# One place modulo 256 bytes for all TensorE operands of a two-network kernel, and offsets of their own for two kinds of tiles

## The chip, the cores and the metric

The kernel runs on 1 core of one Trainium2 chip. The metric is the device time of one execution in microseconds (us). Its profile follows five engines: PE is TensorE's matmul (PEld its weight load), DVE VectorE, ACT ScalarE, POOL GpSimd and SP SyncE.

## The reference

Two networks follow each other, both of depth 2 on 512 tokens of width 1024, all in float32. The first has latent attention and differential attention, each followed by a layer norm and a squared-ReLU MLP of width 4096 with a layer norm. The second has forgetting attention and retention, each followed by a SwiGLU MLP of width 2816, with root-mean-square norms ahead of each part.

```python
def reference(x, positions, ...):
    x = first_block(x, positions, ...)
    return second_block(x, norm_mix_2, ...)

def first_block(x, ...):
    for i in range(2):
        m = _mla(x, ...) if i == 0 else _diff_attn(x, ...)
        x = _layernorm(ALPHA * x + m, ...)
        x = _layernorm(ALPHA * x + square(relu(x @ w_up)) @ w_down, ...)
    return x

# second_block, for each of its two layers:
#   x = x + (forgetting_attention or retention)(rmsnorm(x, g1))
#   x = x + (silu(a) * b) @ w_out,  with  a, b = halves of  rmsnorm(x, g2) @ w_in
# and at last rmsnorm(x, final_norm)
```

## The kernel before

The whole program is one instruction stream for each engine. There are eight stages: mla, f0 (MLP), diff, f1 (MLP), fox, g0 (SwiGLU), ret and g1 (SwiGLU).

**Three products for one.** Every float32 operand is split into two float32r parts, a high and a low one (`split`: ACT copies the high part, DVE subtracts it). `mm3` then issues three TensorE products: high times high, high times low, low times high. The first argument of `matmul` after the output is the stationary operand (128 columns that are loaded into the array), the second the moving one (up to 512 columns that stream through).

**Weights** come from DRAM as chunks of [128, 1024] float32 through two `raw` buffers, and are split into a ring of five `whi` and five `wlo` tiles (`get`, `done`).

**Feature-major products** (`fgemm`, `ftile`, `fhead`, `proj`): 128 columns of `whi` or `wlo` are stationary, and the normed tokens `XH` or `XL` (features on partitions, 512 tokens) move. One output tile takes 8 k-tiles of three products. `fhead` does the first four tiles of a stage in halves of 256 tokens: the first halves need the token tiles 0 and 1 alone, the second halves the tiles 2 and 3.

**Token-major products** (`tgemm`, made of `t_first` and `t_second`, and `v_half`): 128 tokens are stationary, 512 columns of a weight chunk move. In an MLP the stationary operands are `jh` and `jl`: `jit` splits two k-tiles of the hidden layer (`h` or `z`) just in time, with 3 buffers in f0 and f1 and 4 in g0 and g1. `t_second` takes most chunks in the order chunk, then token tile. The last `lr` chunks (3 in f0 and f1, 4 in g0 and g1) it takes in the order token tile, then chunk, so that a token tile is finished every 6 `lr` products. Each finished token tile goes through its norm (`ln_fin` or `rms_fin`: `add` and `a` on DVE, ACT and POOL), then through 8 transposes on PE and a split into `XH` and `XL` (`to_xT`), for the `fhead` of the next stage.

**Order.** A list scheduler at build time gives each engine its order: the instruction that comes first in the program among those that are ready. A tile of a pool is handed to a new user when all users of the former one are done. So an instruction that needs a buffer still in use is passed by later ones.

**Where tiles lie.** A tile takes a byte range of its own in every partition, rounded up to 32 bytes, and tiles follow one another in the order of their pools. The sizes of nearly all tiles are multiples of 256 bytes. Exceptions move what comes behind them: `mh` (16 bytes) and `col` (64) lie between `XH`, `XL` and the weight ring; four tiles `ss` of 8 bytes lie ahead of `jh` and `jl` in g0 and g1, and ahead of ret's tiles; three small tiles in diff, and `bf`, `rc` in fox, lie ahead of the attention's tiles. The four `st` tiles of 48 bytes take 256 together.

Of the kernel before, what the change touches and what calls it, by code (L numbers as in the profile page):

```python
# [9 lines left out]
F32 = mybir.dt.float32  # L10
F32R = mybir.dt.float32r
# [4 lines left out]
PSUM = bass.MemoryType.PSUM  # L16

D = 1024
S = 512
NT = 4  # L20
# [8 lines left out]
AUTO = True  # L29
# how much of the tensor engine's other work (ns) is put before what waits for a chain of the  # L30
# other engines, and how many products of that work go with each query tile
PLAN = {
# [8 lines left out]
class Net:  # L41
    def __init__(self, ctx, tc, A):
        self.tc, self.nc, self.A = tc, tc.nc, A
        nc = self.nc
        self.cst = ctx.enter_context(tc.tile_pool(name="cst", bufs=1))
        self.wp = ctx.enter_context(tc.tile_pool(name="wp", bufs=1))
        self.sm = ctx.enter_context(tc.tile_pool(name="sm", bufs=1))
        self.pp = ctx.enter_context(tc.tile_pool(name="pp", bufs=8, space=PSUM))
        c = self.cst
        self.X = c.tile([128, NT, D], F32, name="X")  # L50
        self.XH = c.tile([128, 8, S], F32R, name="XH")
        self.XL = c.tile([128, 8, S], F32R, name="XL")
        self.idn = c.tile([128, 128], F32, name="idn")
        self.mask = c.tile([128, S], F32, name="mask")
        self.mh = c.tile([128, 4], F32, name="mh")
        self.col = c.tile([128, 16], F32, name="col")
        self.seq = []
        self.n_dma = self.n_split = self.n_get = self.n_done = 0
        self.raw, self.sp = {}, {}
        self.fq = []  # L60
        self.unit = 0
        self.rt = self.tables = None
        self.late = {}
        self.owed = 0
        self.clk, self.dq, self.busy = 0.0, [], False

    def ps(self, name="ps"):
        return self.pp.tile([128, 512], F32, tag="ps", name=name)

    def small(self, n, name):  # L70
        return self.sm.tile([128, 8], F32, tag="small", name=name, bufs=24)[:, 0:n]

    # weight stream: every chunk is [128, n] of float32, split into two float32r parts
    def dma_next(self, eng=None):
# [46 lines left out]

    # work behind a chain of the other engines is issued only after enough of the tensor
    # engine's other work: clk counts what the tensor engine was given, in ns
    def defer(self, delay, fn):
# [33 lines left out]

    # features on partitions: out[m, tok] over kts k-tiles, weights stationary
    def fgemm(self, ps, w, off, kts, xh, xl, n0=0, n1=S, m=128):  # L160
# [5 lines left out]

    # the first tiles after a norm run in token halves, so that the norm's tail is hidden
    def fhead(self, n, evac):
# [35 lines left out]
    def mm_t(self, ps, t, lh, ll, w, first, last):  # L204
        # two k-tiles of a [128 tok, 512] product
        ts = slice(t * 128, t * 128 + 128)
        for j in range(2):
            ws = slice(j * 512, j * 512 + 512)
            self.mm3(ps, lh[:, j, ts], ll[:, j, ts], w[0][:, ws], w[1][:, ws], first and j == 0, last and j == 1)

    # tokens on partitions: out[tok, 1024] in two column halves, lhs(c) -> (hi, lo) [128, 2, 512]
    def t_first(self, nch, lhs, fin0, ahead=True):
# [17 lines left out]
    def t_second(self, nch, lhs, lr, fin_a, fin_b, strict, pre=None):  # L230
        fin = []
        b = [self.ps("tb") for _ in range(NT)]
        L = pre or {0: lhs(0)}
# [48 lines left out]

    # one 512-column half of a normed [128, 1024] token tile into xT
    def to_xT(self, src, t, g):
# [56 lines left out]
    def rms_fin(self, pool, g, dst=None):  # L341
        nc = self.nc
        X = [self.halves(self.X[:, t, :]) for t in range(NT)]
        G = self.halves(g)
        ss = [pool.tile([128, 2], F32, name=f"ss{t}", bufs=1) for t in range(NT)]
        out = {}
# [22 lines left out]
    def jit(self, pool, src, bufs, tags=("jh", "jl"), ready=None):  # L369
        def lhs(c):  # L370
            if ready is not None:
                self.need(lambda: ready() > 2 * c + 1)
            h = pool.tile([128, 2, S], F32R, tag=tags[0], name="jh", bufs=bufs)
            l = pool.tile([128, 2, S], F32R, tag=tags[1], name="jl", bufs=bufs)
            self.split(h, l, src[:, 2 * c:2 * c + 2, :])
            return h, l
        return lhs

    # causal softmax numerators of [128 q, keys] in PSUM; sum into rs
    def softmax(self, pool, s, qt, tag, sm, scale=1.0):  # L380
# [22 lines left out]

    # out^T [dv, q] = sum over keys of V^T P^T; V is [tok, head, (tile, dv)], and the result takes
    # the place of its head's values as [dv, head, (tile, q)]
    def pv(self, VH, VL, h, PH, PL):
# [6 lines left out]

    # heads cut into query tiles: scores of one tile, other work for the tensor engine, and the
    # transposes and values behind the chains of the softmax
    def attend(self, pool, heads, scores, VH, VL, post, fills):
# [25 lines left out]

    # rotary embedding with features on partitions; swap names, in each group of 32 partitions, the
    # partner of a feature
    def rope(self, pool, src, swap, C, Sn):
# [8 lines left out]

    # cos and signed sin of positions * inv, features on partitions
    def rope_tables(self, pool, tmp, which, tags=("t0", "t1", "t2"), bufs=1):
# [212 lines left out]

    # attention, its output projection and the norm behind it  # L670
    def attn_out(self, outer, p, scores, VH, VL, nready, post, fills, gname, bname, row):
# [15 lines left out]
    def ffn1(self, i):  # L687
        nc, A, tc = self.nc, self.A, self.tc
        with ExitStack() as es:
            p = es.enter_context(tc.tile_pool(name="f_a", bufs=1))  # L690
            h = p.tile([128, 32, S], F32, name="h")
            g = self.bcast(p, A["ln_ffn_g"][i:i + 1, :], D, "g")
# [9 lines left out]
            for m in range(4, 32):  # L702
                evac(m, self.ftile())
                if m == 8 and i == 0:
                    self.tables = self.rope_tables(self.rt, p, 1, ("ntmp",) * 3, 4)
            self.tgemm(16, self.jit(p, h, 3), 3, self.ln_fin(p, g, bb, g2))

# [6 lines left out]

    # one 512-column half of a token-major projection: 4 chunks of two k-tiles
    def v_half(self, VH, VL, dst):
# [11 lines left out]
    def diff(self):  # L728
        nc, A, tc = self.nc, self.A, self.tc
        mm = nc.tensor.matmul  # L730
        with ExitStack() as outer:
# [3 lines left out]
            p = outer.enter_context(tc.tile_pool(name="d_a", bufs=1))  # L735
            nlam = p.tile([128, 1], F32, name="nlam")
            sub = p.tile([128, 1], F32, name="sub")
            ones = p.tile([128, 2], F32, name="ones")
            with tc.tile_pool(name="d_0", bufs=1) as p0:
# [18 lines left out]
            def evac(h, which):  # L758
                def f(ps):
                    r = self.rope(p, ps, DIFF_SWAP, C, Sn)  # L760
                    # a sub-head's queries lie above their low parts, its keys twice: one product of full
                    # height gives two of the three parts
                    if which == 0:
# [24 lines left out]
            def scores(h, qt):  # L788
# [3 lines left out]
                if qt == 0:  # L792
                    s1[h] = p.tile([128, 4], F32, tag="s1", name="s1", bufs=3)
                q, k, kl = qk[h]
# [18 lines left out]
            def post(h, o):  # L813
# [6 lines left out]
                def sums():  # L820
# [5 lines left out]
                    nc.vector.tensor_copy(s8, sps[:, 0:8])  # L826
                    # the values lack the division by the sum of the first softmax; so does eps
                    nc.vector.tensor_tensor(rr, s1[h], s1[h], op=ALU.mult)
# [19 lines left out]
    def fox(self):  # L848
        nc, A, tc = self.nc, self.A, self.tc
        mm = nc.tensor.matmul  # L850
        with ExitStack() as outer:
# [3 lines left out]
            pa = p = outer.enter_context(tc.tile_pool(name="x_a", bufs=1))  # L855
            bf = p.tile([32, 1], F32, name="bf")
            nc.gpsimd.dma_start(out=bf, in_=A["fox_b"])
            rc = p.tile([32, 16], F32, name="rc")
            nc.gpsimd.dma_start(out=rc, in_=A["c_rows"])
# [194 lines left out]
    def ffn2(self, i):  # L1054
        nc, A, tc = self.nc, self.A, self.tc
        n = DFF2 // 128
        with ExitStack() as es:
# [15 lines left out]
            for m in range(4, 2 * n):  # L1073
                evac(m, self.ftile())
            self.tgemm(n // 2, self.jit(p, z, 4), 4, self.rms_fin(p, g, A["out"] if i == 1 else None))

# [29 lines left out]
def body(tc, A, phases=PHASES, auto=AUTO):  # L1106
    with ExitStack() as ctx:
# [8 lines left out]
        for ph in phases:  # L1116
            net.plan = PLAN[ph]
            if ph in ("f0", "diff") and net.rt is None:
# [23 lines left out]
def pack_v(w):  # L1142
    # 512 columns, two k-tiles a chunk
    return w.reshape(-1, 2, 128, 512).transpose(0, 2, 1, 3).reshape(-1, 128, 1024)


def pack_h(w):
    # two 512-column halves, each in chunks of two k-tiles
    return np.concatenate([pack_v(np.ascontiguousarray(w[:, :512])), pack_v(np.ascontiguousarray(w[:, 512:]))])


# rotary features of the latent attention, the two halves side by side in each group of 32
ROPE_ORDER = np.array([16 * (i // 32) + i % 16 + 32 * (i % 32 // 16) for i in range(64)])
# [110 lines left out]
```

## Time and profile before

| | us |
|---|---|
| median of 2 runs (2596.21 and 2596.28) | 2596.24 |
| span of the profiled execution, first to last instruction | 2594.1 |
| time around that span (median less span) | 2.1 |
| PE busy | 2561.4 |
| DVE busy | 1289.7 |
| ACT busy | 929.4 |
| POOL busy | 170.4 |

Busy time counts a product from its start to its modelled end, and the products overlap: what a product costs in a row of others is the distance from its start to the next one's start, not its duration. The profiled execution's own time outside its span isn't listed, so sums are made in the span and carried over to the median one to one.

### The profile page before, as it was taken

The numbers are of one execution on the slowest core, as the hardware profiler recorded it, in microseconds if no ns is written. First come the engines' busy times: TensorE is split into PE (matmuls) and PEld (weight loads), VectorE is DVE, ScalarE is ACT, GpSimd is POOL, SyncE is SP. The second block draws the span as 40 slices with busy tenths as digits, with TensorE's granted clock in tenths as the row PEclk, the third lists the DMA queues.
The fourth block names the chain that finished last, engine by engine and source line by source line (L and its number), as shares of the span: only waits on it lengthen the run. The fifth ranks groups of instructions, "written<-read, shape, count | busy, mean of one in ns | idle before, by whom it ended". The sixth has DMA issues, their size and how long they took to land.

```text
span 2594.1 us, 30292 instructions
## 1 busy us (share of the span) xinstructions
PE 2561.4 (99%) x12164; PEld 2100.7 (81%) x12164; DVE 1289.7 (50%) x1961; ACT 929.4 (36%) x1416; POOL 170.4 (7%) x238
## 2 busy tenths in 40 slices
PE   8999999999999999999999999999999999999998
PEld 7778888887778888887778888888888888888887
DVE  6865334566986333546455432244455544432243
ACT  5634223335663323334443322233322233322232
POOL 1100000012431000003000000000000000000000
PEclk9999999999999999999999999999999999999999
DMA  4213323323122322232211322222322222322322
GB/s 153 98 49 126 98 90 98 98 76 98 58 65 90 98 98 90 98 98 84 74 57 49 119 93 97 90 96 91 112 77 85 77 82 81 106 98 90 98 90 74
DMA packets 65837, 233.05 MB, mean 90 GB/s; under 512 B 7536, under 2 KB 7680, under 8 KB 65696
## 3 DMA queue, kind: packets, MB, share of 16 engines
q1 hardware_dynamic: 62064, 219.21, 25.8%
q0 software_dynamic: 3488, 11.55, 1.4%
q8 instruction: 95, 1.56, 0.3%
q14 instruction: 46, 0.38, 0.0%
q10 hardware_dynamic: 144, 0.36, 0.0%
HBM read 228.99 MB, written 2.10 MB: 89 GB/s over the span
## 4 chain that ended last, share of the span: by engine, by line
PE 54%; POOL 0%; issue 0%; ACT 0%; DVE 0%; DVEq 0%; POOLq 0%; ACTq 0%
PE ps L151 8%; PE ps L152 8%; PE ps L150 8%; PE ta L150 2%; PE ta L152 2%; PE ta L151 2%; PE tb L152 2%; PE tb L151 2%; PE tb L150 2%; PE pj L150 2%; PE v L150 2%; PE v L152 2%; PE pj L152 2%; PE pj L151 2%; PE v L151 2%; PE tp L156 1%
## 5 line engine op out<-in xcount | busy, mean ns | idle before, releaser
L117 DVE TENSOR_TENSOR wlo<-raw,whi 128x1024 fp32r<-128x1024 f32 (+2 forms) x415 | 507.6, 1225 | 535.1 <-ACT whi L116 530.5
L116 ACT CAST whi<-raw 128x1024 fp32r<-128x1024 f32 (+2 forms) x415 | 431.4, 1041 | 878.2 <-PE ps L151 578.5
L150 PE MATMUL ps<-XH,whi 128*128 128x512 f32 (+1 forms) x1664 | 609.7, 367 | 2.1 <-ACT XH L116 2.1
L151 PE MATMUL ps<-XL,whi 128*128 128x512 f32 (+1 forms) x1664 | 608.8, 366 | 0.2 <-DVE XL L117 0.2
L152 PE MATMUL ps<-XH,wlo 128*128 128x512 f32 (+1 forms) x1664 | 608.5, 366 | 0.0
L150 PEld LDWEIGHTS ps<-XH,whi 128*128 128x128 f32 x1664 | 314.2, 189 | 57.7 <-ACT XH L116 2.3
L151 PEld LDWEIGHTS ps<-XL,whi 128*128 128x128 f32 x1664 | 314.4, 189 | 56.0 <-DVE XL L117 0.7
L152 PEld LDWEIGHTS ps<-XH,wlo 128*128 128x128 f32 x1664 | 314.3, 189 | 55.8
L150 PE MATMUL ta<-whi,jh 128*128 128x512 f32 x496 | 194.6, 392 | 0.0
L152 PE MATMUL ta<-whi,jl 128*128 128x512 f32 x496 | 194.3, 392 | 0.0
L151 PE MATMUL ta<-wlo,jh 128*128 128x512 f32 x496 | 194.3, 392 | 0.0
L150 PE MATMUL tb<-whi,jh 128*128 128x512 f32 x448 | 176.5, 394 | 0.0
L152 PE MATMUL tb<-whi,jl 128*128 128x512 f32 x448 | 175.6, 392 | 0.0
L151 PE MATMUL tb<-wlo,jh 128*128 128x512 f32 x448 | 175.6, 392 | 0.0
L117 DVE TENSOR_TENSOR jl<-h,jh 128x1024 fp32r<-128x1024 f32 x64 | 78.4, 1225 | 174.8 <-ACT jh L116 174.8
L116 ACT CAST jh<-h 128x1024 fp32r<-128x1024 f32 x64 | 67.6, 1056 | 205.7 <-PE ta L151 110.8
L150 PE MATMUL pj<-XH,whi 128*128 128x512 f32 x288 | 121.2, 421 | 0.0
L152 PE MATMUL pj<-XH,wlo 128*128 128x512 f32 x288 | 114.3, 397 | 0.0
L151 PE MATMUL pj<-XL,whi 128*128 128x512 f32 x288 | 113.8, 395 | 0.0
L152 PEld LDWEIGHTS ta<-whi,jl 128*128 128x128 f32 x496 | 93.3, 188 | 20.6
L151 PEld LDWEIGHTS ta<-wlo,jh 128*128 128x128 f32 x496 | 93.3, 188 | 20.3
L150 PEld LDWEIGHTS ta<-whi,jh 128*128 128x128 f32 x496 | 93.3, 188 | 20.3
(325 smaller groups left out, 3612.2 us busy)
## 6 DMA issues: line engine op xcount, KB each, us to landing
raw<-in_w_in SPq DMA_DIRECT2D x88, 512.0 KB, 3.3
raw<-in_w_up SPq DMA_DIRECT2D x64, 512.0 KB, 3.3
raw<-in_w_dn SPq DMA_DIRECT2D x64, 512.0 KB, 3.3
raw<-in_w_r SPq DMA_DIRECT2D x48, 512.0 KB, 3.3
raw<-in_w_out SPq DMA_DIRECT2D x44, 512.0 KB, 3.3
raw<-in_w_d SPq DMA_DIRECT2D x24, 512.0 KB, 3.3
raw<-in_w_x SPq DMA_DIRECT2D x24, 512.0 KB, 3.3
raw<-in_w_ro SPq DMA_DIRECT2D x16, 512.0 KB, 3.3
```

The lines of the kernel that those rows point to most:

```text
L116: nc.scalar.copy(hi, src)
L117: (eng or nc.vector).tensor_tensor(lo, src, hi.bitcast(F32), op=ALU.subtract)
L150: mm(ps, ah, bh, start=first, stop=False)
L151: mm(ps, ah, bl, start=False, stop=False)
L152: mm(ps, al, bh, start=False, stop=last)
L156: self.nc.tensor.transpose(out, src, self.idn)
```

## The change

It does four things.

1. Tiles whose size is no multiple of 256 bytes are padded or gathered, so that all tiles that TensorE reads begin at one place modulo 256 bytes: `mh` and `col` become parts of one tile of 256 bytes, `ss` takes 64 bytes, the small tiles of diff and fox go into one tile `few` of 256 bytes, `s1` moves to the pool of small tiles, whose other tag goes from 24 to 21 buffers.
2. `XH` and `XL` get 64 more columns (256 bytes), and are views into their tiles that begin `PLACE[stage]` elements of 4 bytes behind the tile's start. `t_second` sets the place of the next stage before its norm writes.
3. `jh` and `jl` of the MLPs get 64 more columns too, and begin `JIT[stage]` elements behind the start of their tile.
4. `jit` gets one buffer less: 2 in f0 and f1, 3 in g0 and g1. `lr` stays at 3 and 4.

```diff
+PLACE = {"f0": 8, "diff": 16, "f1": 48, "fox": 60, "g0": 56, "ret": 4, "g1": 2}
+JIT = {"f0": 4, "f1": 16, "g0": 8, "g1": 48}
...
-        self.XH = c.tile([128, 8, S], F32R, name="XH")
-        self.XL = c.tile([128, 8, S], F32R, name="XL")
+        self.xh = c.tile([128, 8 * S + 64], F32R, name="XH")
+        self.xl = c.tile([128, 8 * S + 64], F32R, name="XL")
+        self.place("mla")
...
-        self.mh = c.tile([128, 4], F32, name="mh")
-        self.col = c.tile([128, 16], F32, name="col")
+        mc = c.tile([128, 64], F32, name="mc")
+        self.mh, self.col = mc[:, 0:4], mc[:, 16:32]
...
+    def place(self, ph):
+        o = PLACE.get(ph, 0)
+        self.XH, self.XL = (x[:, o:o + 8 * S].rearrange("p (k n) -> p k n", k=8) for x in (self.xh, self.xl))
...
-        return self.sm.tile([128, 8], F32, tag="small", name=name, bufs=24)[:, 0:n]
+        return self.sm.tile([128, 8], F32, tag="small", name=name, bufs=21)[:, 0:n]
...
     def t_second(self, nch, lhs, lr, fin_a, fin_b, strict, pre=None):
         fin = []
+        i = PHASES.index(self.stage) + 1
+        if i < len(PHASES):
+            self.place(PHASES[i])
...
-        ss = [pool.tile([128, 2], F32, name=f"ss{t}", bufs=1) for t in range(NT)]
+        ss = [pool.tile([128, 16], F32, name=f"ss{t}", bufs=1) for t in range(NT)]
...
-            h = pool.tile([128, 2, S], F32R, tag=tags[0], name="jh", bufs=bufs)
-            l = pool.tile([128, 2, S], F32R, tag=tags[1], name="jl", bufs=bufs)
+            if self.stage == "ret":
+                h, l = (pool.tile([128, 2, S], F32R, tag=n, name="jh", bufs=bufs) for n in tags)
+            else:
+                o = JIT[self.stage]
+                h, l = (pool.tile([128, 2 * S + 64], F32R, tag=n, name=n, bufs=bufs)[:, o:o + 2 * S].rearrange("p (k n) -> p k n", k=2) for n in tags)
...
-            self.tgemm(16, self.jit(p, h, 3), 3, self.ln_fin(p, g, bb, g2))
+            self.tgemm(16, self.jit(p, h, 2), 3, self.ln_fin(p, g, bb, g2))
...
-            self.tgemm(n // 2, self.jit(p, z, 4), 4, self.rms_fin(p, g, A["out"] if i == 1 else None))
+            self.tgemm(n // 2, self.jit(p, z, 3), 4, self.rms_fin(p, g, A["out"] if i == 1 else None))
...
-            net.plan = PLAN[ph]
+            net.plan, net.stage = PLAN[ph], ph
```

The rest gathers the small tiles of diff and fox in the same manner, moves `s1`, and blanks comment lines.

## Rows read from the trace of the kernel before

**Rows 1.** The page: span, and busy time of the engines.

```profile
span 2594.1 us, 30292 instructions
PE 2561.4 (99%) x12164; PEld 2100.7 (81%) x12164; DVE 1289.7 (50%) x1961; ACT 929.4 (36%) x1416; POOL 170.4 (7%) x238
```

**Rows 2.** Timeline of PE: where f0's feature-major and token-major stretches begin.

```profile
223.31 0.39 PE L150 MATMUL ps<-XH,whi 128*128 128x512 f32 x1
...
380.75 0.40 PE L150 MATMUL ta<-whi,jh 128*128 128x512 f32 x1
...
467.80 0.39 PE L150 MATMUL tb<-whi,jh 128*128 128x512 f32 x1
```

**Rows 3.** The same timeline: both ends of g0's first token-major half.

```profile
1678.24 0.39 PE L150 MATMUL ta<-whi,jh 128*128 128x512 f32 x1
...
1739.58 0.40 PE L150 MATMUL tb<-whi,jh 128*128 128x512 f32 x1
```

**Rows 4.** The same timeline: a value projection of ret, first product and what follows.

```profile
1827.21 0.39 PE L150 MATMUL v<-whi,XH 128*128 128x512 f32 x1
...
1849.61 0.39 PE L150 MATMUL at<-H 128*128 128x512 f32 x1
```

**Rows 5.** Groups by line and shape, PE, whole span: count, busy us, mean ns.

```profile
L150 PE MATMUL ps<-XH,whi 128*128 128x512 f32 x1216 | 482.2, 397 | 0.0
L150 PE MATMUL ta<-whi,jh 128*128 128x512 f32 x496 | 194.6, 392 | 0.0
L150 PE MATMUL tb<-whi,jh 128*128 128x512 f32 x448 | 176.5, 394 | 0.0
L150 PE MATMUL ps<-XH,whi 128*128 128x256 f32 x448 | 127.5, 285 | 2.1 <-ACT XH L116 2.1
L150 PE MATMUL pj<-XH,whi 128*128 128x512 f32 x288 | 121.2, 421 | 0.0
L150 PE MATMUL v<-whi,XH 128*128 128x512 f32 x256 | 102.6, 401 | 2.0 <-DVE VL L117 2.0
```

**Rows 6.** Timeline of PE: end of f0 and start of diff.

```profile
556.45 0.40 PE L152 MATMUL tb<-whi,jl 128*128 128x512 f32 x1
...
559.39 0.38 PE L151 MATMUL ps<-XL,whi 128*128 128x256 f32 x1
```

**Rows 7.** Timeline of DVE at the same end: norms of two token tiles.

```profile
542.80 0.69 DVE L310 SCALAR_TENSOR_TENSOR X<-X,tb 128x512 f32<-128x512 f32 x1 [0.86 <-PE tb L152]
...
547.71 0.68 DVE L310 SCALAR_TENSOR_TENSOR X<-X,tb 128x512 f32<-128x512 f32 x1
```

**Rows 8.** Timeline of DVE at f1's end: norms of two token tiles.

```profile
1167.87 0.68 DVE L310 SCALAR_TENSOR_TENSOR X<-X,tb 128x512 f32<-128x512 f32 x1
...
1174.51 0.68 DVE L310 SCALAR_TENSOR_TENSOR X<-X,tb 128x512 f32<-128x512 f32 x1
```

**Rows 9.** Timeline of PE: last work of f1 and first product of fox.

```profile
1179.74 1.04 PE L156 MATMUL tp<-idn,nt 128*128 128x128 f32 x8
1182.85 0.50 PE L150 MATMUL ps<-XH,whi 128*128 128x256 f32 x2 [2.07 <-ACT XH L116]
```

**Rows 10.** Stretches of fox's start: PE busy (products), granted clock.

```profile
1184.00:1186.40 2.40, 2.40 (x13) 0.50 0.00 0
1188.00:1190.00 2.00, 2.00 (x20) 1.00 0.00 0
```

**Rows 11.** Timeline: PE's first product of ret, DVE's last norm in g1.

```profile
1802.66 0.28 PE L150 MATMUL ps<-XH,whi 128*128 128x256 f32 x1
...
2587.08 0.69 DVE L349 TENSOR_TENSOR X<-X,tb 128x512 f32<-128x512 f32 x1 [1.50 <-PE tb L152]
...
2589.74 1.41 DVE L358 SCALAR_TENSOR_TENSOR nt<-X,rs,g 128x512 f32<-128x512 f32 x2 [1.97 <-POOL rs L270]
```

**Rows 12.** The tile jh: split of a chunk on ACT and DVE, min/median/max ns.

```profile
L116 ACT CAST jh<-h x64: 1043/1057/1057, 222.2 to 1158.7; 128x1024 fp32r<-128x1024 f32 x64
L117 DVE TENSOR_TENSOR jl<-h,jh x64: 1216/1226/1226, 223.5 to 1159.7; 128x1024 fp32r<-128x1024 f32 x64
```

More of the change, by code (lines that the diff above doesn't have):

```diff
@@ L735, in diff @@
             p = outer.enter_context(tc.tile_pool(name="d_a", bufs=1))
-            nlam = p.tile([128, 1], F32, name="nlam")
-            sub = p.tile([128, 1], F32, name="sub")
-            ones = p.tile([128, 2], F32, name="ones")
+            few = p.tile([128, 64], F32, name="few")
+            nlam, sub, ones = few[:, 0:1], few[:, 8:9], few[:, 16:18]
             with tc.tile_pool(name="d_0", bufs=1) as p0:
@@ L792, in scores @@
                 if qt == 0:
-                    s1[h] = p.tile([128, 4], F32, tag="s1", name="s1", bufs=3)
+                    s1[h] = self.sm.tile([128, 8], F32, tag="s1", name="s1", bufs=3)[:, 0:4]
                 q, k, kl = qk[h]
@@ L855, in fox @@
             pa = p = outer.enter_context(tc.tile_pool(name="x_a", bufs=1))
-            bf = p.tile([32, 1], F32, name="bf")
+            few = p.tile([32, 64], F32, name="few")
+            bf, rc = few[:, 0:1], few[:, 16:32]
             nc.gpsimd.dma_start(out=bf, in_=A["fox_b"])
-            rc = p.tile([32, 16], F32, name="rc")
             nc.gpsimd.dma_start(out=rc, in_=A["c_rows"])
```

## The prediction

> **What bounds the kernel now.** I read the page first: PE is busy for 2561.4 of 2594.1 us, so all other engines are covered by it and only 32.7 us are left in which PE has nothing to do [rows 1]. The time can fall through PE alone: through shorter distances from product to product, or through fewer waits.
>
> Second, the timeline of PE, for the distance between the starts of neighbouring products of 512 columns. [...] In f0 the feature-major part from 223.31 to 380.75 holds 672 products: 157.44 us / 672 = 234.3 ns. The token-major half behind it, 380.75 to 467.80, holds 384: 87.05 / 384 = 226.7 ns [rows 2]. The same kind of half in g0, 264 products in 61.34 us, takes 232.3 ns [rows 3]. A value projection of ret, 96 products in 22.40 us, takes 233.3 ns [rows 4]. No wait stands in any of these stretches.
>
> Third, I worked out from the code where the operands lie modulo 256 bytes. Between `XH`, `XL` and the weight ring stand `idn` (512), `mask` (2048), `mh` (16, rounded to 32) and `col` (64): the ring lies 96 bytes further on. In f0 and f1 only multiples of 256 stand between the ring and `jh`, `jl`: the same place. In g0, g1 and ret the four `ss` of 8 bytes take 32 each: `jh` lies 128 bytes behind the ring's place. While one product streams its moving operand, the stationary operand of the next one is read. Distance of the two, moving less stationary: 0 gives 226.7 ns, +96 (values) 233.3, 128 (g0) 232.3, and -96 (feature-major) 234.3. So I take it that the place modulo 256 bytes matters, and that 0 is the best of the four that have long undisturbed stretches.
>
> **The change part by part.** *Operands brought together.* After the change all bases are at one place, so the distances are the offsets alone: feature-major +32 bytes in f0, +64 in diff, -64 (192) in f1, -16 (240) in fox, -32 (224) in g0, +16 in ret, +8 in g1; token-major in the MLPs -16, -64, -32 and +64 (-192). None of these has a long stretch in the trace. [...] All lie within 64 bytes of 0, most within 32, and 0 is nearer to them than 96 is (for 64 it is not). So I take the value of distance 0, 226.7 ns, for all.
>
> The counts come from the groups by line and shape, times the three lines of `mm3` [rows 5]:
> - feature-major, 512 columns: 3 x 1216 = 3648 at 234.3 - 226.7 = 7.6 ns: 27.7 us;
> - projections `pj` between attention, same distance: 3 x 288 = 864 at 7.6: 6.6 us;
> - values `v`: 3 x 256 = 768 at 233.3 - 226.7 = 6.6: 5.1 us;
> - token-major with `jh`: 3 x (496 + 448) = 2832, of which f0 and f1 have 2 x 768 = 1536 at 226.7 already; the other 1296 at 5.6: 7.3 us.
>
> Sum 46.7 us. The 1344 products of 256 columns I leave at nothing: no row has them at distance 0 in a row of their own kind. They would add 0 to some 3 us, and the range takes that in.
>
> [...] The rows say that the rate hangs on the two operands' places [rows 2 to 4]. [...]
>
> *One buffer less for `jh`, `jl`, with `lr` as it was.* In the last `lr` chunks of `t_second` all `lr` splits are alive at once, and now there are only `lr` - 1 buffers. The last chunk's split must wait until the chunk `lr` - 1 places ahead of it has been used by all four token tiles. The list scheduler lets PE go on with what is ready, so all token tiles take the early chunks, and then each takes the last chunk alone: 6 products, 6 x 0.227 = 1.4 us, instead of 18 or 24 (4.1 or 5.4 us). The four norms, which stood 4.1 us or more apart, now begin nearly together at the stage's end, and DVE works them off one by one. Queued behind that: the transposes on PE, and `fhead`, which needs tiles 0 and 1. Token tile 0 is done 4.1 us ahead of the last product.
> - f0 to diff: DVE takes 547.71 - 542.80 = 4.9 us a tile [rows 7]. Tile 1 is normed at -4.1 + 9.8 = 5.7 us after the last product, and in `XH`, `XL` some 2.3 later (8 transposes 1.0 [rows 9], split about 1.3, as one split takes a little over 1 us of DVE for twice 512 columns): 8.0. Today PE is back at 559.39, 2.7 us after the last product's slot [rows 6]. At most +5.3.
> - f1 to fox, where a second norm on POOL and ACT follows: 1174.51 - 1167.87 = 6.6 us a tile, and from tile 1's start on DVE to fox's first product 1182.85 - 1167.87 = 15.0 us [rows 8, 9]. Tile 1 would start at 2.5 and be ready at 17.5; today it is 1182.85 - 1179.74 = 3.1. At most +14.4.
> - g0 to ret: one norm takes 2589.74 + 1.41 - 2587.08 = 4.1 us [rows 11], mostly not on DVE. Tile 1 is ready some 2.8 us ahead of the end plus 4.1 plus 2.3, that is at 3.6, and DVE's doubling adds a little: at most +4, as today ret starts with no wait [rows 11].
> - g1's end: the last tile's norm behind the third's: at most +1.5.
> - in f0 and f1 the last split (1.06 on ACT, 1.23 on DVE [rows 12]) has only 1.4 us of other products above it: 2 x 0.9 = 1.8.
> [...]
>
> Sum of the upper ends: 29.5 us. The lower end is 0: these bounds let DVE do nothing in parallel and take today's latencies with their queueing, and PE's chunks could still be ordered so that tiles 0 and 1 come first. I take a third, 10 us, as the bound of 14.4 counts f1's queueing twice. No steady part pays for the missing buffer: a split takes 2.3 us, and a chunk lasts 24 x 0.227 = 5.4 us [rows 2, 12].
>
> *Offsets themselves, padding, small tiles.* They add no instruction; `small` with 21 buffers has tiles of 32 bytes that live for one norm or softmax. Nothing.
>
> Sum: 46.7 - 10 = 36.7 us off the span, 2594.1 to 2557.4; the median stands 2.1 us above the span, so 2596.2 - 36.7 = 2559.5, say 2559.
>
> **The rivals.** *The offsets do better than 0 (lower).* [...] For it: at 0 both reads begin at one place at the same time, which looks like the worst that two readers can do, and yet it is the best of four. Against it: no stretch comes below 226.7. [...]
>
> *The stage ends eat the gain (slower than before).* The place is the last chunk of the four MLPs, the price 29.5 us. It decides if the gain is below that, 29.5 us / 6576 = 4.5 ns a product: so if offsets of 32 and 64 bytes cost like 96 does. Then only g1 (+8; 960 products), ret and fox (16 bytes) gain, some 13 us, f1's token-major part loses up to 768 x 6 = 4.6 us, and the time is 2596 - 8 + 29.5 = 2617. For it: the rise from 0 to 96 has no row in between.
>
> *The place is not what sets the rate.* The four stretches also differ in which operand moves and in the stage; then nothing is gained, and the time is 2596 + 10 = 2606.
>
> **How the numbers follow.** Forecast 0.50 (2544 to 2594), the lower rival 0.33 (2450 to 2544), the stage ends 0.13 (2594 to 2625), no effect 0.04. The likeliest gives 2559. For 8 in 10 the range leaves out the lowest tenth and the highest tenth: 2488 to 2602. Faster by over 2% means below 2544, the lower rival and a little of the forecast's edge: 0.38. Slower by over 2% would need 2648, above all cases: 0.02. Within 2%: 0.60. (2% is about what a measurement of this kernel can tell from no change.)
>
> **What the changed profile would show.** The timeline of PE: 672 products of f0's feature-major part in 152.3 us instead of 157.4; g0's half of 264 in 59.8 instead of 61.3; f0's token-major half still 87. [...] At f0's end the last chunk's products of the four token tiles would stand together, and PE's waits for `X`, `XH` or `nt` at the starts of diff, fox and ret would grow from 1 to 2 us to between 3 and 15; if the tiles still end 4 us apart, that term is 0. The prediction is wrong if the rate depends on more than the distance, for instance on the start of the moving operand within its 256 bytes, which the change moves too.

## The result, and the profile after

The changed kernel takes 2610.36 us (2 runs, 2609.65 and 2611.07) against 2596.24: ratio 1.0052, 95% interval 1.0033 to 1.0071. It is 14 us slower, where 37 us less were forecast; the time lies above the range.

First the page: span, and busy time of the engines, which answer to [rows 1].

```profile
span 2609.3 us, 30310 instructions
PE 2562.5 (98%) x12164; PEld 2099.8 (80%) x12164; DVE 1288.9 (49%) x1961; ACT 929.7 (36%) x1416; POOL 169.7 (7%) x238
```

PE is busy for 1.1 us more than before, and idle for 2609.3 - 2562.5 = 46.8 us instead of 32.7. So PE's busy time shows nothing of the 46.7 us that the products were to gain, and 14.1 us of new waits have come.

Second the timeline of PE in the changed kernel: f0's feature-major stretch, its first token-major half, and the half of g0, for [rows 2, 3]. Line 158 is line 150 of before; all later lines of helpers move by about as much.

```profile
222.19 0.39 PE L158 MATMUL ps<-XH,whi 128*128 128x512 f32 x1
...
378.99 0.40 PE L158 MATMUL ta<-whi,jh 128*128 128x512 f32 x1
...
468.59 0.40 PE L158 MATMUL tb<-whi,jh 128*128 128x512 f32 x1
...
1695.72 0.40 PE L158 MATMUL ta<-whi,jh 128*128 128x512 f32 x1
...
1757.32 0.40 PE L158 MATMUL tb<-whi,jh 128*128 128x512 f32 x1
```

672 products in 156.80 us are 233.3 ns each (before 234.3, forecast 226.7). 384 in 89.60 are 233.3 (before 226.7, and forecast to stay). 264 in 61.60 are 233.3 (before 232.3, forecast 226.7). All three stand at one rate now, and it is not the rate of distance 0.

Third the waits of PE, us in total, times, longest; the first and fourth group of the view.

```profile
PE tp L164 <- ACT nt L343: 12.0, 3, 6.8
...
PE tp L164 <- DVE X L334: 4.3, 2, 3.2
```

Before, the same waits, for `nt` and for `X` ahead of the transposes, were 2.0 and 1.2 us. Their places are the ends of f0 and f1, in the same timeline:

```profile
558.15 0.40 PE L160 MATMUL tb<-whi,jl 128*128 128x512 f32 x1
559.68 1.32 PE L164 MATMUL tp<-idn,X 128*128 128x128 f32 x8 [1.13 <-DVE X L334]
564.18 1.97 PE L164 MATMUL tp<-idn,X 128*128 128x128 f32 x8 [3.19 <-DVE X L334]
566.70 0.58 PE L159 MATMUL ps<-XL,whi 128*128 128x256 f32 x1
...
1186.10 0.40 PE L160 MATMUL tb<-whi,jl 128*128 128x512 f32 x1
1193.29 1.97 PE L164 MATMUL tp<-idn,nt 128*128 128x128 f32 x8 [6.80 <-ACT nt L343]
1199.80 1.54 PE L164 MATMUL tp<-idn,nt 128*128 128x128 f32 x6 [4.54 <-ACT nt L343]
...
1201.59 0.80 PE L158 MATMUL ps<-XH,whi 128*128 128x256 f32 x2
```

From f0's last product to diff's first product on `XL` it is now 566.70 - 558.15 = 8.6 us (before 2.9, [rows 6]). Behind f1 PE stands still for 6.8 and 4.5 us, and fox's first products stand 1201.59 - 1186.10 = 15.5 us behind f1's last. The timeline of DVE at f1's end shows why: the split of the last chunk, and then the first instruction of each of the four norms, for [rows 8].

```profile
1180.27 1.23 DVE L125 TENSOR_TENSOR jl<-h,jh 128x1024 fp32r<-128x1024 f32 x1 [7.54 <-ACT jh L124]
...
1182.79 0.69 DVE L321 SCALAR_TENSOR_TENSOR X<-X,tb 128x512 f32<-128x512 f32 x1 [0.16 <-PE tb L160]
...
1184.13 0.67 DVE L321 SCALAR_TENSOR_TENSOR X<-X,tb 128x512 f32<-128x512 f32 x1
...
1184.89 0.69 DVE L321 SCALAR_TENSOR_TENSOR X<-X,tb 128x512 f32<-128x512 f32 x1
...
1189.45 0.63 DVE L321 SCALAR_TENSOR_TENSOR X<-X,tb 128x512 f32<-128x512 f32 x1
```

The split ends 4.6 us ahead of the last product. Its high part, on ACT, had waited for 7.90 us until PE was done with an earlier chunk:

```profile
1179.19 1.05 ACT L124 CAST jh<-h 128x1024 fp32r<-128x1024 f32 x1 [7.90 <-PE tb L159]
```

The norms of the first three token tiles begin within 2.1 us; before, the second and the third alone began 6.6 us apart [rows 8].

Behind the wait of 6.8 us the granted clock is 0.50, as it is behind the wait of 2.1 us at fox's start before [rows 9, 10]. The stretch of the first transposes (PE busy, products, granted clock):

```profile
1193.30:1195.30 2.00, 1.96 (x8) 0.50 0.00 0
```

Eight transposes take 1.97 us there; at f1's end before, at a clock of 1.00, they took 1.04 [rows 9].

### The profile page after: what moved, and what is told of

Its sections match the earlier page's. It is cut to its first block, busy times and chain, and to the rows that moved or that the text cites. A ratio compares the mean times of both kernels' runs of the same rounds, so it can differ in the third digit from the quotient of the medians.

```text
span 2609.3 us, 30310 instructions
## 1 busy us (share of the span) xinstructions
PE 2562.5 (98%) x12164; PEld 2099.8 (80%) x12164; DVE 1288.9 (49%) x1961; ACT 929.7 (36%) x1416; POOL 169.7 (7%) x238
## 4 chain that ended last, share of the span: by engine, by line
PE 71%; DVE 3%; POOL 2%; ACT 2%; issue 1%; DMA 0%; DVEq 0%; POOLq 0%; ACTq 0%
PE ps L159 10%; PE ps L158 10%; PE ps L160 10%; PE ta L160 4%; PE ta L158 4%; PE tb L159 4%; PE tb L158 4%; PE ta L159 4%; PE tb L160 4%; PE pj L158 2%; PE v L158 2%; PE v L160 2%; PE v L159 2%; PE pj L159 2%; PE pj L160 2%; PE tp L164 1%
## 5 line engine op out<-in xcount | busy, mean ns | idle before, releaser
L160 PE MATMUL ta<-whi,jl 128*128 128x512 f32 x432 | 169.8, 393 | 0.0
L160 PE MATMUL tb<-whi,jl 128*128 128x512 f32 x432 | 169.0, 395 | 0.0
L125 DVE TENSOR_TENSOR jl<-z,jh 128x1024 fp32r<-128x1024 f32 x44 | 53.9, 1224 | 134.2 <-ACT jh L124 134.2
```

Source lines behind the costliest of these rows:

```text
L125: (eng or nc.vector).tensor_tensor(lo, src, hi.bitcast(F32), op=ALU.subtract)
L160: mm(ps, al, bh, start=False, stop=last)
```

## The experiments

Theory 1, formed on this result: distance 0 does give 226.7 ns and all the small offsets throw it away; the buffers cost what they cost, apart from that. Rivals: the rate rises smoothly with the distance; some place is better than 0; the buffer cut, not the offsets, carries the loss; the missing buffer costs by itself and not through `lr`.

A rate in this section is the time from the first product of a stretch to the first of the next one, over the number of products: feature-major 672 in f0 and f1, 960 in g0 and g1; token-major 384 and 264 in the first half.

**The offsets set to nothing (zero_offsets).** The changed kernel, with its buffers still cut:

```diff
-PLACE = {"f0": 8, "diff": 16, "f1": 48, "fox": 60, "g0": 56, "ret": 4, "g1": 2}
-JIT = {"f0": 4, "f1": 16, "g0": 8, "g1": 48}
+PLACE = {}
+JIT = {'f0': 0, 'f1': 0, 'g0': 0, 'g1': 0}
```

> The changed kernel with all offsets set to 0, so that every distance between the moving operand and the next stationary one is 0; buffers stay cut. Theory 1 (the distance alone sets the rate, 0 is the best place and 226.7 ns hold there for feature-major products too): the some 5900 products that the changed kernel does at 233 ns fall to 226.7, 41 us off 2610, so about 2570; f0's 672 feature-major products in 152.3 us. Rival (feature-major products do not reach 226.7 at any place, what was seen at distance 0 belongs to the token-major form): only f0's and f1's token-major halves gain, 1536 x 6.6 ns = 10 us, about 2600.

Measured 2572.67 us, ratio to before 0.9905 (0.9889 to 0.9922). The offsets alone cost 2610.4 - 2572.7 = 38 us (39 by the spans, 2609.3 against 2570.2). Timeline of PE in f0:

```profile
222.36 0.40 PE L158 MATMUL ps<-XH,whi 128*128 128x512 f32 x1
...
374.71 0.39 PE L158 MATMUL ta<-whi,jh 128*128 128x512 f32 x1
...
461.75 0.39 PE L158 MATMUL tb<-whi,jh 128*128 128x512 f32 x1
```

672 products in 152.35 us and 384 in 87.04: 226.7 ns in both forms; no other long stretch of this kernel without a wait is more than 0.3 ns away from that. The waits are those of the changed kernel (12.3 us for `nt`). The two buffers of `jh` are 4352 bytes long here, 17 times 256, so one of them lies 256 bytes off the ring modulo 512, and the 384 products keep their 226 to 227 ns all through: 256 bytes apart gave the rate of 0.

**The buffers given back too (zero_full).** Without the offsets the 64 extra columns aren't needed, and there is room for 3 and 4 buffers:

```diff
-        self.xh = c.tile([128, 8 * S + 64], F32R, name="XH")
+        self.xh = c.tile([128, 8 * S], F32R, name="XH")
...
-            self.tgemm(16, self.jit(p, h, 2), 3, self.ln_fin(p, g, bb, g2))
+            self.tgemm(16, self.jit(p, h, 3), 3, self.ln_fin(p, g, bb, g2))
...
-            self.tgemm(n // 2, self.jit(p, z, 3), 4, self.rms_fin(p, g, A["out"] if i == 1 else None))
+            self.tgemm(n // 2, self.jit(p, z, 4), 4, self.rms_fin(p, g, A["out"] if i == 1 else None))
```

(`XL`, `jh` and `jl` lose their 64 columns in the same way.)

> The same with the buffers of jh and jl back at 3 and 4, and without the 64 extra columns. Theory 1 with the stage ends as the cause of the other loss (PE idles 14 us more in the changed kernel than before): 14 us less than zero_offsets, about 2556. Rival (the stage ends wait for the norms whatever the buffers): as zero_offsets within 3 us.

Measured 2554.05 us, ratio 0.9834 (0.9820 to 0.9849): the fastest version of the study, ahead of both kernels. The buffers bring back 18.6 us where 14 were expected. Its page, and its waits for `nt`:

```profile
span 2555.1 us, 30294 instructions
...
PE 2520.5 (99%) x12164; PEld 2100.3 (82%) x12164; DVE 1289.4 (50%) x1961; ACT 928.5 (36%) x1416; POOL 170.3 (7%) x238
...
PE tp L164 <- ACT nt L343: 2.8, 2, 2.0
```

PE's busy time falls by 2561.4 - 2520.5 = 40.9 us; idle are 34.6 us, 1.9 more than before. That is the prediction's first term, on a kernel that has the alignment, the padding that goes with it, and nothing else.

**The buffers cut in the kernel before (before_bufs).**

```diff
-            self.tgemm(16, self.jit(p, h, 3), 3, self.ln_fin(p, g, bb, g2))
+            self.tgemm(16, self.jit(p, h, 2), 3, self.ln_fin(p, g, bb, g2))
...
-            self.tgemm(n // 2, self.jit(p, z, 4), 4, self.rms_fin(p, g, A["out"] if i == 1 else None))
+            self.tgemm(n // 2, self.jit(p, z, 3), 4, self.rms_fin(p, g, A["out"] if i == 1 else None))
```

> The kernel before with one edit: jh and jl have 2 buffers in f0 and f1 and 3 in g0 and g1. Theory: the stage ends alone cost what the changed kernel lost, 14 us: 2610, with PE's waits at the starts of diff, fox and ret as in the changed kernel. Rival (the loss comes from f0's and f1's token-major halves, 1536 products at 6.6 ns more, and the ends cost a few us): 2596 to 2600.

Measured 2615.27 us, ratio 1.0068 (1.0053 to 1.0083). Waits of PE:

```profile
PE tp L156 <- ACT nt L332: 12.0, 3, 6.8
...
PE tp L156 <- DVE X L323: 4.4, 2, 3.2
```

These are the changed kernel's waits, without any change of place. The cut costs 2615.3 - 2597.5 = 17.8 us at the old places and 2572.7 - 2554.1 = 18.6 at distance 0: two effects that add up. The rival that the buffers carry the whole loss is out: 18 us are a third of the 56 that lie between zero_full and the changed kernel.

**The ends, one pair at a time (zero_f3).** zero_offsets without the 64 columns, and with the third buffer back in f0 and f1 alone:

```diff
-            self.tgemm(16, self.jit(p, h, 2), 3, self.ln_fin(p, g, bb, g2))
+            self.tgemm(16, self.jit(p, h, 3), 3, self.ln_fin(p, g, bb, g2))
```

> The aligned kernel with the third buffer given back in f0 and f1 alone; g0 and g1 stay at 3 buffers with lr 4. Theory 1 (the loss lies at the ends of f0 and f1, where PE's gaps of 7.2, 5.0, 3.5 and 1.5 us stand): about 17 of the 18.6 us come back, 2554 to 2558 us. Rival (all four MLPs lose alike): about 2563 us.

Measured 2561.54 us (2559.99 to 2562.53), ratio 0.9864 (0.9849 to 0.9878). 11.1 of the 18.6 us come back, so this expectation missed, and the time lies nearer to the rival's 2563: I had counted the long gaps alone, and g0 and g1 keep 7.5 us by the medians (4.4 by the spans, 2559.5 against 2555.1). PE's gaps at ret's start are only about 1 us long, but g1's last norm also ends later, 9.8 us behind its last product instead of 7.5. The medians can't tell 11.1 from an even half of the loss; the stages, taken apart below, show that f1 loses most.

**`lr` cut with the buffers (zero_lr, zero_lr2).** zero_lr is zero_offsets with

```diff
-            self.tgemm(16, self.jit(p, h, 2), 3, self.ln_fin(p, g, bb, g2))
+            self.tgemm(16, self.jit(p, h, 2), 2, self.ln_fin(p, g, bb, g2))
...
-            self.tgemm(n // 2, self.jit(p, z, 3), 4, self.rms_fin(p, g, A["out"] if i == 1 else None))
+            self.tgemm(n // 2, self.jit(p, z, 3), 3, self.rms_fin(p, g, A["out"] if i == 1 else None))
```

> The aligned kernel with the cut buffers (2572.7 us), and lr cut with them, to 2 in the squared-ReLU MLPs and 3 in the SwiGLU ones. Theory 1 (the 18.6 us are lost because lr late chunks have only lr - 1 buffers, so that all token tiles wait for the last chunk and end together): the token tiles end apart again, 12 or 18 products or 2.7 and 4.1 us instead of 4.1 and 5.4, so most of the loss comes back: 2556 to 2564 us, PE's wait for nt at most 5 us instead of 12. Rival (one buffer less costs by itself, through splits that start later in every chunk): 2571 to 2575.

Measured 2558.59 us, ratio 0.9848 (0.9832 to 0.9864). But with so few late chunks the due time of the norm's tail, 7000 ns in f0, falls behind diff's first products, which by the code therefore read f0's input of token tile 1, still in `XH` and `XL`. That part of the computation is changed and a wait is missing, so 2558.6 is too low to judge by. zero_lr2 restores the order:

```diff
-    "f0": dict(ln=7000), "f1": dict(ln=8500), "g0": dict(ln=5500), "g1": dict(ln=5500),
+    "f0": dict(ln=5500), "f1": dict(ln=5500), "g0": dict(ln=5500), "g1": dict(ln=5500),
```

> The aligned kernel with the cut buffers (2572.7 us) and lr cut with them, to 2 in the squared-ReLU MLPs and 3 in the SwiGLU ones, with the due time of the norm tail (ln) in f0 and f1 lowered to 5500 ns so that diff's first products again come behind token tile 1's norm. Theory 1 (the loss comes from lr late chunks with lr - 1 buffers): most of the 18.6 us come back, 2557 to 2565 us, PE's wait for nt at most 9 us. Rival (a buffer less costs by itself): 2570 to 2575.

Measured 2562.47 us, ratio 0.9868 (0.9853 to 0.9883); the wait for `nt` is 0.1 us above the most that was expected:

```profile
PE tp L164 <- ACT nt L343: 9.1, 4, 4.0
```

**The same `lr` with full buffers (full_lr).** zero_full with the `ln` of zero_lr2 and

```diff
-            self.tgemm(16, self.jit(p, h, 3), 3, self.ln_fin(p, g, bb, g2))
+            self.tgemm(16, self.jit(p, h, 3), 2, self.ln_fin(p, g, bb, g2))
...
-            self.tgemm(n // 2, self.jit(p, z, 4), 4, self.rms_fin(p, g, A["out"] if i == 1 else None))
+            self.tgemm(n // 2, self.jit(p, z, 4), 3, self.rms_fin(p, g, A["out"] if i == 1 else None))
```

> The aligned kernel with its full buffers (3 and 4; 2554 us), but with lr 2 and 3 and the same ln of 5500 ns in f0 and f1. Theory 1 (token tiles that end 2.7 and 4.1 us apart instead of 4.1 and 5.4 leave less cover for the norms of tiles 0 and 1): 2555 to 2565 us, about as long as the cut buffers with the same lr; the spare buffer then does nothing. Rival (the spare buffer saves time by itself at equal lr): at least 5 us below the cut buffers with the same lr.

Measured 2561.07 us, ratio 0.9862 (0.9845 to 0.9878). At equal `lr` the spare buffer is worth 1.4 us, which the intervals don't tell from nothing; at the larger `lr` it is worth 18.6. So, of the settings tried, the buffer is missed where `lr` exceeds the number of buffers. Matching `lr` to the buffers, with the lower `ln`, brings 10.2 us back; the other 7 to 8 are the price of the shorter `lr` and the lower `ln` together, as full_lr shows against zero_full (2561.1 against 2554.1). That the token tiles then end closer together would explain it; no run parts `lr` from `ln`.

**All places moved together (common32).** zero_full with a tile of 32 bytes ahead of all others:

```diff
+        self.pad = c.tile([128, 8], F32, name="pad")
         self.X = c.tile([128, NT, D], F32, name="X")
```

> All operands of the aligned kernel with its buffers restored (2554 us) lie 32 bytes further on together, so that every distance stays 0. Theory 1 (what counts is the distance of the two operands modulo 256 bytes): nothing changes, long stretches at 226.7 ns from product to product, 2551 to 2558 us. Rival (what counts is the absolute place of the operands modulo 256 bytes; +32 of one of them gave 233.3): about 8100 products at up to 6.6 ns more, up to 2607 us.

Measured 2555.25 us, ratio 0.9834 (0.9819 to 0.9849). Timeline of PE in f0 (the added line makes 158 line 159):

```profile
223.10 0.40 PE L159 MATMUL ps<-XH,whi 128*128 128x512 f32 x1
...
375.44 0.39 PE L159 MATMUL ta<-whi,jh 128*128 128x512 f32 x1
...
462.48 0.39 PE L159 MATMUL tb<-whi,jh 128*128 128x512 f32 x1
```

672 products in 152.34 us and 384 in 87.04: 226.7 ns, as without the 32 bytes. At distance 0, moving both operands by 32 bytes changes nothing; at other distances no run moves them together.

**Other offsets (scan_a, scan_b, scan_c, same_off).** These are the changed kernel with other values in `PLACE` and `JIT`, one execution each. `PLACE` is in elements of 4 bytes, and so is `JIT`, which moves the stationary operand and so counts the other way; 60 is -16 bytes in `PLACE` and +16 in `JIT`.

```diff
+PLACE = {'f0': 1, 'f1': 63, 'g0': 62, 'g1': 3}
+JIT = {'f0': 63, 'f1': 58, 'g0': 54, 'g1': 52}
```

> The changed kernel with other offsets, one distance for each long stretch. Feature-major +4 bytes in f0, -4 in f1, -8 in g0, +12 in g1; token-major +4 in f0, +24 in f1, +40 in g0, +48 in g1; 0 elsewhere. Theory 1 in its narrow form (only 0 locks at 226.7): all eight stretches between 228 and 234 ns. Rival a (the rate rises smoothly with the distance): +4 and -4 within 1 ns of 226.7, 48 above 230. Rival b (a place better than 0 exists): one of the eight below 226 ns.

```diff
+PLACE = {'f0': 14, 'f1': 18, 'g0': 20, 'g1': 28}
+JIT = {'f0': 28, 'f1': 20, 'g0': 12, 'g1': 59}
```

> The changed kernel with other offsets: feature-major stretches at +56 (f0), +72 (f1), +80 (g0), +112 bytes (g1), token-major at +144, +176, +208 and +20. Theory 1 (distance 0 is the best place, a few others equal it, none is below it): every long stretch between 226.5 and 238 ns, the time between 2585 and 2612. Rival (some place beats 0): at least one stretch below 226 ns.

```diff
+PLACE = {'f0': 10, 'f1': 60, 'g0': 6, 'g1': 12}
+JIT = {'f0': 56, 'f1': 1, 'g0': 2, 'g1': 61}
```

> The changed kernel with distances that the token-major or the feature-major products have run at before, now in the other form: feature-major +40 (f0), -16 (f1), +24 (g0), +48 (g1); token-major +32, -4, -8 and +12. Theory 1 (the distance alone sets the rate, whichever operand was moved): feature-major 226.7 at +40, 231.1 at +24, 233.3 at +48; token-major 233.3 at +32, 230.6 at -4, 232.0 at -8, 228.9 at +12, each within 0.5 ns. Rival (the start of the moving operand within its 256 bytes counts as well, as the 237.9 at +4 against 233.3 suggests): at least half of the eight differ by 1 ns or more.

```diff
+PLACE = {'f0': 1, 'f1': 1, 'g0': 1, 'g1': 1}
+JIT = {'f0': 4, 'f1': 4, 'g0': 4, 'g1': 4}
```

> The changed kernel with one offset for each form in all four MLPs: feature-major +4 bytes (237.9 ns in f0 before), token-major -16 (233.3 in f0 before, but 226.7 for the last three value projections of ret at the same distance). Theory 1 (form and distance together set the rate): the four feature-major stretches agree within 0.5 ns at 237.9, the four token-major ones at 233.3, the time 2612 to 2622. Rival (what went before counts too, so that one place has several rates): at least two of the eight stretches differ from the others of their form by 1 ns or more.

They took 2599.55, 2603.87, 2609.64 and 2627.12 us. Two stretches of scan_a, f0's feature-major one at +4 bytes and g0's token-major one at +40:

```profile
223.03 0.41 PE L158 MATMUL ps<-XH,whi 128*128 128x512 f32 x1
...
382.93 0.39 PE L158 MATMUL ta<-whi,jh 128*128 128x512 f32 x1
...
1693.41 0.39 PE L158 MATMUL ta<-whi,jh 128*128 128x512 f32 x1
...
1753.25 0.39 PE L158 MATMUL tb<-whi,jh 128*128 128x512 f32 x1
```

672 products in 159.90 us are 237.9 ns, the slowest of all, four bytes away from the best. 264 in 59.84 are 226.7: a second place as good as 0. In scan_c the same +40 in the other form, f0's feature-major stretch:

```profile
222.84 0.39 PE L158 MATMUL ps<-XH,whi 128*128 128x512 f32 x1
...
378.88 0.39 PE L158 MATMUL ta<-whi,jh 128*128 128x512 f32 x1
```

156.04 us, 232.2 ns. So the same distance has different rates in the two forms. The forms differ in two things, in what streams and in which operand was moved out of the common place, and no run parts these. And in same_off, +4 and -16 in f0 and again in g1:

```profile
223.66 0.41 PE L158 MATMUL ps<-XH,whi 128*128 128x512 f32 x1
...
383.56 0.40 PE L158 MATMUL ta<-whi,jh 128*128 128x512 f32 x1
...
473.16 0.40 PE L158 MATMUL tb<-whi,jh 128*128 128x512 f32 x1
...
2264.24 0.40 PE L158 MATMUL ps<-XH,whi 128*128 128x512 f32 x1
...
2492.65 0.40 PE L158 MATMUL ta<-whi,jh 128*128 128x512 f32 x1
...
2554.25 0.40 PE L158 MATMUL tb<-whi,jh 128*128 128x512 f32 x1
```

159.90 / 672 and 228.41 / 960 are 237.9 ns; 89.60 / 384 and 61.60 / 264 are 233.3. Over four stages each form keeps its rate within 0.05 ns: in these stretches form and distance together set it. (The whole took 2627 where 2612 to 2622 were expected. I had set the sum too low: 2 x 672 + 2 x 960 = 3264 feature-major products at 4.6 ns above 233.3 are 15 us on top of the changed kernel's 2610.) All rates of 512-column products, ns from product to product, from before, the changed kernel and the experiments:

| distance, bytes | feature-major | token-major (`jh`) |
|---|---|---|
| 0 | 226.7 | 226.7 |
| +4 / -4 | 237.9 / 230.6 | 233.3 / 232.4 |
| +8 / -8 | 232.8 / 232.0 | - / 230.7 |
| +12 | 228.9 | 233.3 |
| -16 | 236.7 | 233.3 |
| +20 | - | 231.7 |
| +24 | 234.2 | 231.1 |
| +32 / -32 | 233.3 / 233.3 | 233.3 / 233.3 |
| +40 | 232.2 | 226.7 |
| +48 / -48 | 233.3 / - | 233.3 / 233.3 |
| +56 | 232.2 | - |
| +64 / -64 | - / 233.3 | 229.0 / 233.3 |
| +72 | 235.5 | - |
| +80 / -80 | 231.1 / - | - / 232.0 |
| -96 | 234.3 | - |
| +112 / -112 | 231.1 / - | - / 233.3 |
| 128 | - | 232.3 |

No entry is below 226.7: for 512 columns the rival that some place beats 0 found nothing. The smooth rise is out (+4 is the worst). That 0 is the only good place is out too (+40). That the distance alone decides, whatever the form, is out: of the eight pairs that scan_c was made for, six differ by more than 1 ns, and only +32 and +48 agree.

For the products of 256 columns, 0 is not the best place. Timeline of PE at f1's start, 132 of them in a row, in the changed kernel (-64 bytes) and in zero_offsets (0):

```profile
835.08 0.37 PE L158 MATMUL ps<-XH,whi 128*128 128x256 f32 x1
...
850.03 0.28 PE L160 MATMUL ps<-XH,wlo 128*128 128x256 f32 x1
```

```profile
825.16 0.36 PE L158 MATMUL ps<-XH,whi 128*128 128x256 f32 x1
...
840.95 0.28 PE L160 MATMUL ps<-XH,wlo 128*128 128x256 f32 x1
```

From the first start to the last these are 14.95 us / 131 = 114.1 ns at -64 and 15.79 / 131 = 120.5 at 0. With 512 columns the order is the other way round, 233.3 and 226.7.

## Why the prediction was wrong, point by point

**What bounds the kernel: right.** PE is the end of it in all versions, and every difference was found in its products or its waits.

**The place matters, and 0 is the best of the four: right.** The alignment by itself moves PE's busy time by 40.9 us and the median by 2597.5 - 2554.1 = 43.4, against the 46.7 of the sum; that also rules out the rival by which the place sets nothing. In the table, where only the two operands' places differ, the rate goes from 226.7 to 237.9 ns. That a product and the load of the next stationary operand begin together, as the prediction has it, the trace of before shows: at 400.03 us, at distance 0, a product starts and with it the next one's load, PEld for 0.19 us. The 1344 products of 256 columns, left at nothing with 0 to 3 us to gain, gain nothing: their long rows took 117.9 to 120.6 ns before and take 120.5 to 120.6 at distance 0.

**"For all I take the value of distance 0": the step that failed.** It stood on "0 is nearer to them than 96 is", that is, on a rate that changes little over a few tens of bytes. The runs show that 4 bytes can change it from the best rate of the table to the worst. Of the offsets with a long stretch, those of f0, f1 and g0 run at 233.3, and only g1's token-major +64 (229.0) and some of the value projections come nearer to 226.7. The four feature-major stretches gain 0.6, 0.6, 0.9 and 1.5 us on before instead of 5.1 in f0 and in f1 and 7.3 in g0 and in g1; the first token-major halves of f0 and f1, at distance 0 before, lose 2.55 us each. The offsets cost 38 us, of a gain of 43. The prediction had named a part of this, that 32 and 64 bytes cost like 96, and gave it 0.13; that +8 and -16 bytes lose nearly all of it too, none of its cases had.

**One buffer less: the mechanism right, the size taken too low.** The order of the last chunk and the norms that begin together came as described; the term was 10 us and measured 18 (0 to 29.5 were its bounds). I had taken a third, because f1's bound seemed to count its queueing twice. Between the first token-major products of f0, f1, g0 and g1 and the end, the spans of zero_offsets and zero_full differ by 2.5 (f0), 7.5 (f1), 3.2 (g0) and 2.6 us (g1). They add up to 15.8 and not to 18.6, as the profiled execution of zero_full was its slowest. The bounds were 5.3, 14.4, 4 and 1.5, with 1.8 more for splits: half of the first two, most of the third, and more than the fourth. The last 2.5 us of the 29.5 stood for a lower clock at two stage ends; no run shows that term by itself. The changed kernel shows a granted clock of 0.50 behind the waits at the ends of f0 (564.10 to 566.20 us) and f1, and at each of them eight transposes of 1.97 us, 0.9 more than the 1.04 at a clock of 1.00. At f1's end the queueing was real: fox's first products come 15.5 us behind the last product, where the bound had 17.5. But in zero_full, as before, token tile 0's transposes and a wait of 2.0 us for them stood among f1's last products, and they have moved into the long wait: f1's second token-major half, from its first product to its last, takes 87.2 us in zero_offsets and 90.1 in zero_full. At g1's end the last norm starts 1.4 us behind the last product instead of 0.4, behind three others.

**The rival that was named on the slower side: right in the main.** "The stage ends eat the gain" had its condition met in f0, f1 and g0, as 32 and 64 bytes cost there nearly what 96 does, and the result lies in its range. Its 2617 is 7 us too high: the ends cost 18 and not 29.5, and the products gained 43 - 38 = 5 us and not 8, as g1's feature-major stretch at +8 gave 1.5 us where 960 x 7.6 ns = 7.3 were counted.

**The lower rival: not seen.** No stretch of 512 columns is below 226.7 ns. Its range of 2450 to 2544 us needs products below that; how short one can be was my assumption, and no run shows it.

**Padding and small tiles: nothing,** as said: zero_full has them all but the 64 columns, and PE is idle there for only 1.9 us more than before.

## What to carry to other kernels

When the rate of products hangs on where operands lie, take each address that a change makes as a case of its own: four bytes moved 226.7 to 237.9 ns here, and no row between two measured places stands for its neighbour. Bring both operands to one place modulo 256 bytes first, which gained 43 us in a kernel made mostly of 512-column products, and look from product to product in each form and width before adding anything to it. Before a buffer is given up, count who holds it at the end of a stage: here a loop that keeps `lr` chunks alive wanted `lr` buffers. One less cost 17.8 us in before_bufs, and the price appeared mostly in the next stage's first waits: those for `nt` and `X` went from 2.0 and 1.2 us to 12.0 and 4.4.

## What the hardware showed that I had not expected

- Two rates come back again and again: 226.7 and 233.3 ns, both at a granted clock of 1.00 (before from 380.75 to 467.80 us, the changed kernel from 222.19 to 378.99). The stretches at 226.7 are constant from product to product, at 226 or 227 ns, and so is f1's token-major 233.3 at -64, at 233 or 234. f0's 233.3 at +32 is a mean over products between 230 and 236 ns, its 237.9 at +4 over 232 to 243.
- The value projections of ret in the changed kernel, which have the weights moving and the tokens stationary, at distance -16. In the first head 96 products follow products of 256 columns, in the second feature-major ones of 512:

```profile
1848.37 0.39 PE L158 MATMUL v<-whi,XH 128*128 128x512 f32 x1
...
1870.76 0.39 PE L158 MATMUL at<-H 128*128 128x512 f32 x1
...
1928.02 0.39 PE L158 MATMUL v<-whi,XH 128*128 128x512 f32 x1
...
1930.74 0.60 PE L164 MATMUL tp<-idn,yn 128*128 128x128 f32 x4
1931.10 0.48 PE L158 MATMUL v<-whi,XH 128*128 128x512 f32 x1
...
1949.55 0.39 PE L158 MATMUL at<-H 128*128 128x512 f32 x1
```

The 96 of the first head take 22.39 us, 233.2 ns each. In the second, 12 products from its fourth on take 2.72 us, 226.7 ns, and behind four transposes the last 81 take 18.45 us, 227.8 ns with the restart in it. So at one distance two rates are possible, though `jh` at -16 kept 233.3 in all four MLPs of same_off. What picks one of them, and what makes +40 good in one form and not in the other, stays open.
